# Split-weight stores issued by GpSimd instead of SyncE, and a scan that writes its own first column instead of a GpSimd copy

## The chip, the cores and the metric

The kernel runs on one core of a Trainium2 chip. A core has five engines, each with its own queue of instructions that it works through in order: TensorE (PE in the profile; its weight loads are PEld), VectorE (DVE), ScalarE (ACT), GpSimd (POOL) and SyncE (SP, which here only issues DMAs). Engines wait for one another through semaphores. DMAs move data between HBM and the on-chip memory SBUF; matmuls write to PSUM. A DMA is issued by an engine's queue (here SyncE, ScalarE or GpSimd) and runs beside the engines. The metric is device time in microseconds (us) of one execution; lower is better.

## The reference

A two-layer decoder trunk on x of 2048 positions by 1024 channels, float32. Layer 0 is a gated short convolution, layer 1 a stick-breaking attention with 8 heads of 64:

```python
def _short_conv_mixer(h, w_in, w_conv, w_out):
    u = h @ w_in                                   # 1024 -> 4096
    b_gate, c_gate, xin, g = jnp.split(u, 4, axis=-1)
    y = b_gate * _causal_depthwise_conv(c_gate * xin, w_conv)   # width 3
    return (y * jax.nn.silu(g)) @ w_out

# attention, per block of 128 queries
z = jnp.einsum("bhqd,bhkd->bhqk", qb, kf[:, :, :kl]) * scale
mask = jnp.arange(kl)[None, :] < q_pos[:, None]
log_one_minus = jnp.where(mask, jax.nn.log_sigmoid(-z), 0.0)
rev = lax.cumsum(log_one_minus, axis=3, reverse=True)
weights = jnp.exp(jnp.where(mask, z + rev, -jnp.inf))
outs.append(jnp.einsum("bhqk,bhkd->bhqd", weights, vf[:, :, :kl]))
```

The whole is: x plus mixer of RMSNorm(x); k and v from a RMSNorm of that; q and a SiLU gate from another RMSNorm; x plus the gated attention output times w_out_b; a last RMSNorm. Since exp(z + rev) is sigmoid(z) times the product of sigmoid(−z) over the later keys, a weight is one sigmoid times a running product. The kernel stores positions in reverse, so the running product goes from the low column to the high one.

## The kernel before

Channels lie on the 128 partitions, positions in four chunks of 512 columns (`CH`). Matmuls run in three passes: each weight and each activation is split into a high part (rounded to fp32r) and a low part (the rest), and `mm3` (L205) multiplies high by high, high by low and low by high: 24 matmuls of 128x128 by 128x512 for a depth of 1024.

*Weights.* `load_raw` (L176) loads a block of 128 columns of a weight matrix from HBM, 512 KB, into one of two raw buffers (`NRAW`); its DMA is line L180. `split` (L172) makes the high part on ScalarE (L173) and the low part by a subtraction on VectorE, or on GpSimd for w_out_b (L174). `split_w` (L188) does this into a tile `whl`, one of four (`NWB`), and then writes the split tile, 1 MB (512 KB for w_out_b), to HBM with a DMA on SyncE's queue (L194). Every later use of the block loads the split form back (L202). A block is split once: 8 each for the four gates C, X, B and G of the mixer, 8 each for w_kv and w_in_b (`fold_gains`, which multiplies the norm's gain in first, L366), 8 for w_out_a and 8 for w_out_b, 64 in all. A `whl` buffer is free again when its matmuls are done and its store has landed; a raw buffer is free when its split is done.

*Mixer.* `mixer_in` goes over 8 blocks of channels; for each it computes the gates C, X, B, G of one chunk, or of chunks 0 and 1 together in the first stage, in which all those weights are split. One such block for two chunks is called a round in the prediction. The convolution's tile `p` takes two extra columns from the chunk before: GpSimd copies them in from `halo` (L334) and out to it (L335). The squares for the first norms of chunks 0 and 1 are summed on GpSimd (L170).

*Attention.* `attention(c, h, ot)` handles chunk c of queries and head h; it goes over key chunks `kc` from c down to 0 and over four blocks `qi` of 128 queries. ScalarE makes R = sigmoid(−z) (L489) and w = sigmoid(z) (L491) from PSUM. R is one of five buffers (`NR`) of 513 columns: columns 1 to 512 hold sigmoid(−z), column 0 the product carried in. On the diagonal (kc = c) GpSimd masks R and w (L495) and sets the first column to 1 (L497); off the diagonal it copies the carry, the last column of the R of the key chunk before, into column 0 (L499). VectorE turns columns 1 to 512 into running products with a scan (L500) and multiplies w by R shifted by one column (L504). Then TensorE transposes w (L512), ScalarE and VectorE split the result into `wth` and `wtl` (L173, L174), and TensorE multiplies both by v into `av` (L521, L522). With five buffers, the R of one scan takes the buffer of the R whose last column served as carry to the scan just ahead.

*Out.* `gated` multiplies by the gate on GpSimd (L568), `out_b` projects with w_out_b, adds the residual on VectorE (L591) and sums squares on GpSimd (L170), `out_norm` scales the result on GpSimd (L610).

*Order.* The work is written as Python generators that `merge` interleaves by planned costs; a scheduler then fixes each engine's order from its own timing model of the program as built. Each queue keeps that order on the chip, so an instruction that waits holds up everything behind it on the same engine. Stages follow one another: the mixer of chunks 0 and 1 with all weight splits (to about 400 us), then projections of one chunk beside the mixer of the next and attention of earlier chunks (to about 1400 us), then attention of the last chunk beside the out projections.

Of the kernel before, what the change touches and what calls it, by code (L numbers as in the profile page):

```python
# [8 lines left out]
F32 = mybir.dt.float32  # L9
# [3 lines left out]
ALU = mybir.AluOpType  # L13

P = 128
# [4 lines left out]
CH = 512  # L20
# [25 lines left out]
def kernel(  # L46
# [15 lines left out]
    nc = tc.nc  # L62
# [8 lines left out]
    ones = const.tile([P, P], F32, name="ones")  # L71
# [100 lines left out]
    def split(hi, lo, src, eng=nc.vector):  # L172
        nc.scalar.copy(hi, src)  # L173
        eng.tensor_sub(lo, src, hi.bitcast(F32))  # L174
# [8 lines left out]
    def w_tile(nm, kt=KD):  # L183
        return sb.tile([P, 2, kt, P], F32R, name=f"whl_{nm}", tag="whl", bufs=NWB)


    split_d = {}

    def split_w(raw, key, nm, kt=KD, eng=nc.vector):

        wt = w_tile(nm, kt)
        split(wt[:, 0], wt[:, 1], raw, eng)
        split_d[key] = dram.tile([P, 2, kt, P], F32, name=f"sw_{nm}")
        nc.sync.dma_start(out=split_d[key], in_=wt.bitcast(F32))  # L194
        return wt

    def load_w(src, key, nm, kt=KD, eng=nc.vector):

        if key not in split_d:
            return split_w(load_raw(src, nm, kt), key, nm, kt, eng)  # L200
        wt = w_tile(nm, kt)
        nc.sync.dma_start(out=wt.bitcast(F32), in_=split_d[key])  # L202
        return wt
# [157 lines left out]
    def fold_gains():  # L361

        for nm, src, gain in (("kv", w_kv, gains["kv"]), ("b", w_in_b[0], gains["b"])):
            for i in range(KD):
                raw = load_raw(src[:, i * P:(i + 1) * P], f"fold_{nm}{i}")
                nc.vector.tensor_mul(raw, raw, gain.unsqueeze(2).to_broadcast([P, KD, P]))  # L366
                split_w(raw, (nm, i), f"{nm}{i}")
                yield 1.0
# [96 lines left out]
    def attention(c, h, ot):  # L465

        hb, hi_ = divmod(h, 2)
        nm0 = f"{c}_{h}"
        q2 = sb.tile([P, 2, CH], F32R, name=f"q2_{nm0}", tag="q2", bufs=2)
        for i in range(2):  # L470
            nc.scalar.dma_start(out=q2[i * 64:(i + 1) * 64, :, :].bitcast(F32), in_=q_d[c][hb][hi_ * 64:(hi_ + 1) * 64, :, :])
        av = psum.tile([P, CH], F32, name=f"av_{nm0}", tag="av", bufs=NAV)
        carry = [None] * 4
        for kc in range(c, -1, -1):
            nm = f"{nm0}_{kc}"
            diag = kc == c
            kt = sb.tile([P, CH], F32R, name=f"kt_{nm}", tag="kt", bufs=2)
            nc.scalar.dma_start(out=kt.bitcast(F32), in_=k_d[kc][h])
            vt = sb.tile([P, 4, 2, 64], F32R, name=f"vv_{nm}", tag="vv", bufs=2)
            nc.scalar.dma_start(out=vt.bitcast(F32), in_=v_d[kc][:, :, h, :, :])  # L480
            ws = []
            for qi in range(4):
                lo = qi * P if diag else 0
                lom = min(lo, 256)
                ps = psum.tile([P, CH], F32, name=f"z_{nm}_{qi}", tag="z", bufs=NZ)
                nc.tensor.matmul(ps[:, lom:CH], q2[:, 0, qi * P:(qi + 1) * P], kt[:, lom:CH], start=True, stop=False)  # L486
                nc.tensor.matmul(ps[:, lom:CH], q2[:, 1, qi * P:(qi + 1) * P], kt[:, lom:CH], start=False, stop=True)
                R = sb.tile([P, CH + 1], F32, name=f"R_{nm}_{qi}", tag="R", bufs=NR)
                nc.scalar.activation(R[:, lo + 1:CH + 1], ps[:, lo:CH], AF.Sigmoid, scale=-0.125)  # L489
                w = sb.tile([P, CH], F32, name=f"w_{nm}_{qi}", tag="w", bufs=NW)  # L490
                nc.scalar.activation(w[:, lo:CH], ps[:, lo:CH], AF.Sigmoid, scale=0.125)  # L491
                if diag:

                    for blk, fill in ((R[:, lo + 1:lo + 1 + P], 1.0), (w[:, lo:lo + P], 0.0)):
                        nc.gpsimd.affine_select(out=blk, in_=blk, pattern=[[1, P]], base=0, channel_multiplier=-1,  # L495
                                                compare_op=ALU.is_gt, fill=fill)
                    nc.gpsimd.memset(R[:, lo:lo + 1], 1.0)  # L497
                else:
                    nc.gpsimd.tensor_copy(R[:, 0:1], carry[qi])  # L499
                nc.vector.tensor_tensor_scan(out=R[:, lo + 1:CH + 1], data0=R[:, lo + 1:CH + 1],  # L500
                                             data1=ones[:, 0:1].to_broadcast([P, CH - lo]),
                                             initial=R[:, lo:lo + 1] if diag else carry[qi], op0=ALU.mult, op1=ALU.mult)
                carry[qi] = R[:, CH:CH + 1]
                nc.vector.tensor_mul(w[:, lo:CH], w[:, lo:CH], R[:, lo:CH])  # L504
                ws.append(w)
                yield (1400.0 if diag else 1800.0) / 4
            for kb in range(3, -1, -1):
                nq = kb + 1 if diag else 4
                n = max(256, nq * P)
                wt = psum.tile([P, CH], F32, name=f"wt_{nm}_{kb}", tag="wt", bufs=NWT)  # L510
                for qi in range(nq):
                    nc.tensor.transpose(wt[:, qi * P:(qi + 1) * P], ws[qi][:, kb * P:(kb + 1) * P], ident)  # L512
                first, final = diag and kb == 3, kc == 0 and kb == 0
                wh = sb.tile([P, CH], F32R, name=f"wth_{nm}_{kb}", tag="wth", bufs=NWTS)
                wl = sb.tile([P, CH], F32R, name=f"wtl_{nm}_{kb}", tag="wtl", bufs=NWTS)
                if nq == 1:
                    nc.gpsimd.memset(wh[:, P:2 * P].bitcast(F32), 0.0)
                    nc.gpsimd.memset(wl[:, P:2 * P].bitcast(F32), 0.0)
                split(wh[:, 0:nq * P], wl[:, 0:nq * P], wt[:, 0:nq * P])
                vs = vt[:, kb, :, :].rearrange("p a d -> p (a d)")  # L520
                nc.tensor.matmul(av[:, 0:n], vs, wh[:, 0:n], start=first, stop=False)  # L521
                ins = nc.tensor.matmul(av[:, 0:n], vs, wl[:, 0:n], start=False, stop=final)  # L522
                anchors.append(ins)
                if kb:
                    yield (1900.0 if diag else 3500.0) / 4
            if kc == 0:
                osl = slice(hi_ * 64, hi_ * 64 + 64)
                oth = slice(64 - hi_ * 64, 128 - hi_ * 64)
                nc.scalar.copy(ot[osl, :], av[oth, :])
                nc.vector.tensor_add(ot[osl, :], ot[osl, :], av[osl, :])  # L530
            yield (1900.0 if diag else 3500.0) / 4

    def attention_chunk(c, gated=True):
        for hb in range(NH // 2):
            ot = sb.tile([P, CH], F32, name=f"ot_{c}_{hb}", tag="ot", bufs=2)
            yield from attention(c, 2 * hb, ot)
            yield from attention(c, 2 * hb + 1, ot)
            nc.sync.dma_start(out=og_d[c][hb], in_=ot)
# [168 lines left out]
    def heads(lo, hi, c):  # L707
        for hb in range(lo, hi):
            ot = sb.tile([P, CH], F32, name=f"ot_{c}_{hb}", tag="ot", bufs=2)
            yield from attention(c, 2 * hb, ot)  # L710
            yield from attention(c, 2 * hb + 1, ot)
            if hb == 3:
                last_ot.append(ot)
            else:
                nc.sync.dma_start(out=og_d[c][hb], in_=ot)
# [15 lines left out]
    lo, hi = range(0, NB), range(NB, KD)  # L731
# [34 lines left out]
```

## Time and profile before

| quantity | value |
|---|---|
| median of 3 runs | 1909.28 us (1908.41 to 1910.37) |
| profiled execution | 1907.57 us, its span 1905.8 us |
| TensorE busy | 1784.0 us, 94% of the span |
| VectorE busy | 1264.6 us, 66% |
| ScalarE busy | 769.7 us, 40% |
| GpSimd busy | 436.2 us, 23% |
| carry copies L499 on GpSimd | 192, 112.3 us |
| scans L500 on VectorE | 320, 372.7 us |
| chain that ended last | TensorE 69%, VectorE 14%, DMA 9%, ScalarE 2%, GpSimd 1% |

The profile is one execution, taken by the hardware profiler; its times are counted from the start of the span. A row of the windows view gives, for one stretch of time, the busy time and the number of instructions of each engine, the clock granted to TensorE, the share of DMA capacity used and GB/s. A row of the waits view says which instruction waited for which: total us, times, longest. A row of the chain of work gives start, duration and the work that was on the path. In rows of groups, `out<-in` names the tiles, then shape, count, busy time, mean ns of one, and idle time before them with what ended it. Where a row has three numbers with slashes, they are the shortest, median and longest duration in ns. In rows of DMA issues the last number is the median time from issue to landing in us.

### The profile page before, as it was taken

Reading aid. Unit: us, or ns where it says so; the run is one execution under the profiler, and the core shown is the slowest. Engines: PE = TensorE matmul, PEld = TensorE weight load, DVE = VectorE, ACT = ScalarE, POOL = GpSimd, SP = SyncE. Lnnn points to the kernel's source line nnn. Section 1 sums busy time; section 2 is a strip of 40 time slices with the busy share of each in tenths; the row PEclk is TensorE's granted clock in tenths of the full one; section 3 lists DMA queues with packets and bytes.
Section 4 is the critical chain, followed back from the end, with each engine's and each line's share of the span. In section 5 each row is a group of like instructions: output and inputs, shape, how many; then the busy total and the mean of one; then the engine's idle time right before and its main releaser. Section 6 shows DMA issues by size and latency. Waiting matters only on the chain.

```text
span 1905.8 us, 24702 instructions
## 1 busy us (share of the span) xinstructions
PE 1784.0 (94%) x8312; PEld 1449.4 (76%) x8312; DVE 1264.6 (66%) x1895; ACT 769.7 (40%) x1481; POOL 436.2 (23%) x822
## 2 busy tenths in 40 slices
PE   7899999999999999999999999999979999878785
PEld 5787777778888888888788888888857788656563
DVE  7644554574334264428888346788897999999996
ACT  6312222241123133314545233444555666565553
POOL 5000000000011021103123112222422224654641
PEclk9999999999999999999999999999999999999897
DMA  9648787798887779776767776655746665877751
GB/s 314 210 150 248 248 254 237 243 312 304 295 284 270 258 237 286 246 262 224 242 211 268 238 253 219 202 175 197 258 144 196 197 199 193 284 225 250 252 177 50
DMA packets 226702, 443.64 MB, mean 233 GB/s; under 512 B 16912, under 2 KB 131600, under 8 KB 199952
## 3 DMA queue, kind: packets, MB, share of 16 engines
q1 hardware_dynamic: 166496, 383.30, 60.0%
q10 hardware_dynamic: 59920, 58.74, 10.9%
q8 instruction: 66, 1.08, 0.2%
q14 instruction: 60, 0.49, 0.1%
q0 software_dynamic: 160, 0.02, 0.1%
HBM read 314.34 MB, written 127.66 MB: 232 GB/s over the span
## 4 chain that ended last, share of the span: by engine, by line
PE 69%; DVE 14%; DMA 9%; issue 4%; ACT 2%; POOL 1%; SPq 0%; ACTq 0%; POOLq 0%; DVEq 0%
PE pX L216 8%; PE po L216 7%; PE pG L216 7%; PE pC L216 7%; PE pB L216 6%; PE pg L216 5%; PE pk L216 5%; PE pq L216 5%; PE pv L216 4%; PE wt L512 4%; DVE R L500 4%; PE av L522 3%; DVE w L504 2%; PE av L521 2%; PE z L486 2%
## 5 line engine op out<-in xcount | busy, mean ns | idle before, releaser
L500 DVE TENSOR_TENSOR_SCAN R<-R,R,ones 128x512 f32<-128x512 f32 x192 | 256.6, 1339 | 11.4 <-ACT R L489 11.1
L489 ACT ACTIVATE R<-z 128x512 f32<-128x512 f32 (+1 forms) x320 | 174.2, 544 | 173.1 <-DVE R L500 78.4
L174 DVE TENSOR_TENSOR wtl<-wt,wth 128x512 fp32r<-128x512 f32 (+1 forms) x320 | 185.6, 600 | 67.2 <-ACT wth L173 66.3
L504 DVE TENSOR_TENSOR w<-w,R 128x512 f32<-128x512 f32 (+1 forms) x320 | 212.2, 671 | 21.3 <-POOL R L499 3.0
L173 ACT CAST wth<-wt 128x512 fp32r<-128x512 f32 (+1 forms) x320 | 160.3, 526 | 160.1 <-PE wt L512 137.4
L216 PE MATMUL pC<-h,whl_C 128*128 128x512 f32 x768 | 197.1, 405 | 14.4 <-ACT whl_C L173 8.3
L216 PE MATMUL pG<-h,whl_G 128*128 128x512 f32 x768 | 186.6, 393 | 9.9 <-ACT whl_G L173 9.9
L499 POOL COPY R<-R 128x1 f32<-128x1 f32 x192 | 112.3, 585 | 360.8 <-DVE R L500 293.3
L216 PE MATMUL pX<-h,whl_X 128*128 128x512 f32 x768 | 187.6, 393 | 6.0 <-ACT cs L320 3.9
L216 PE MATMUL po<-y,whl_o 128*128 128x512 f32 x768 | 187.8, 394 | 2.0 <-DVE x L389 1.3
L512 PE MATMUL wt<-ident,w 128*128 128x128 f32 x1088 | 177.8, 278 | 9.2 <-DVE w L504 5.1
L216 PEld LDWEIGHTS pC<-h,whl_C 128*128 128x128 f32 x768 | 148.2, 195 | 49.4 <-ACT whl_C L173 8.3
L216 PE MATMUL pB<-h,whl_B 128*128 128x512 f32 x768 | 185.6, 392 | 0.0
L216 PEld LDWEIGHTS pG<-h,whl_G 128*128 128x128 f32 x768 | 143.2, 188 | 41.0 <-ACT whl_G L173 11.6
L491 ACT ACTIVATE w<-z 128x512 f32<-128x512 f32 (+1 forms) x320 | 172.7, 543 | 0.5 <-PE wt L512 0.5
L216 PEld LDWEIGHTS pX<-h,whl_X 128*128 128x128 f32 x768 | 142.2, 188 | 37.6 <-ACT cs L320 5.1
L216 PEld LDWEIGHTS po<-y,whl_o 128*128 128x128 f32 x768 | 144.2, 189 | 33.5 <-DVE x L389 1.9
L512 PEld LDWEIGHTS wt<-ident,w 128*128 128x128 f32 x1088 | 138.6, 143 | 38.3 <-DVE w L504 7.2
L216 PEld LDWEIGHTS pB<-h,whl_B 128*128 128x128 f32 x768 | 143.0, 188 | 30.1 <-DVE cv L356 0.4
L522 PE MATMUL av<-wtl,vv 128*128 128x512 f32 (+1 forms) x320 | 129.1, 405 | 36.7 <-DVE wtl L174 36.6
L500 DVE TENSOR_TENSOR_SCAN R<-R,ones 128x512 f32<-128x512 f32 (+3 forms) x128 | 116.1, 913 | 33.8 <-POOL R L495 32.2
L486 PE MATMUL z<-kt,q 128*128 128x512 f32 (+1 forms) x320 | 129.1, 405 | 4.1 <-ACT w L491 3.4
(170 smaller groups left out, 2655.3 us busy)
## 6 DMA issues: line engine op xcount, KB each, us to landing
whl_o<-sw_o SPq DMA_DIRECT2D x24, 1024.0 KB, 5.7
kt<-k_d ACTq DMA_DIRECT2D x80, 256.0 KB, 3.6
vv<-v_d ACTq DMA_DIRECT2D x80, 256.0 KB, 4.0
whl_C<-sw_C SPq DMA_DIRECT2D x16, 1024.0 KB, 5.4
whl_X<-sw_X SPq DMA_DIRECT2D x16, 1024.0 KB, 5.5
whl_B<-sw_B SPq DMA_DIRECT2D x16, 1024.0 KB, 5.5
whl_G<-sw_G SPq DMA_DIRECT2D x16, 1024.0 KB, 5.2
whl_k<-sw_kv SPq DMA_DIRECT2D x16, 1024.0 KB, 5.2
```

The lines of the kernel that those rows point to most:

```text
L173: nc.scalar.copy(hi, src)
L174: eng.tensor_sub(lo, src, hi.bitcast(F32))
L216: ins = nc.tensor.matmul(ps, w[:, k, :], a[:, m, k, :], start=n == 0, stop=n == 3 * kt - 1)
L486: nc.tensor.matmul(ps[:, lom:CH], q2[:, 0, qi * P:(qi + 1) * P], kt[:, lom:CH], start=True, stop=False)
L489: nc.scalar.activation(R[:, lo + 1:CH + 1], ps[:, lo:CH], AF.Sigmoid, scale=-0.125)
L491: nc.scalar.activation(w[:, lo:CH], ps[:, lo:CH], AF.Sigmoid, scale=0.125)
L499: nc.gpsimd.tensor_copy(R[:, 0:1], carry[qi])
L500: nc.vector.tensor_tensor_scan(out=R[:, lo + 1:CH + 1], data0=R[:, lo + 1:CH + 1], data1=ones[:, 0:1].to_broadcast([P, CH - lo]), initial= ...
L504: nc.vector.tensor_mul(w[:, lo:CH], w[:, lo:CH], R[:, lo:CH])
L512: nc.tensor.transpose(wt[:, qi * P:(qi + 1) * P], ws[qi][:, kb * P:(kb + 1) * P], ident)
L521: nc.tensor.matmul(av[:, 0:n], vs, wh[:, 0:n], start=first, stop=False)
L522: ins = nc.tensor.matmul(av[:, 0:n], vs, wl[:, 0:n], start=False, stop=final)
```

## The change

Line 194 issues its DMA on GpSimd's queue. In `attention`, GpSimd sets column 0 of every R to 1, on the diagonal or not, and makes no copy of the carry. The scan covers one column more, from column `lo` in place of `lo + 1`: its initial value (1 on the diagonal, the carry off it) is multiplied by that 1 and written to the first column. The carry is read by the scan alone.

```diff
@@ split_w
         split_d[key] = dram.tile([P, 2, kt, P], F32, name=f"sw_{nm}")
-        nc.sync.dma_start(out=split_d[key], in_=wt.bitcast(F32))
+        nc.gpsimd.dma_start(out=split_d[key], in_=wt.bitcast(F32))
         return wt
@@ attention
-                    nc.gpsimd.memset(R[:, lo:lo + 1], 1.0)
-                else:
-                    nc.gpsimd.tensor_copy(R[:, 0:1], carry[qi])
-                nc.vector.tensor_tensor_scan(out=R[:, lo + 1:CH + 1], data0=R[:, lo + 1:CH + 1],
-                                             data1=ones[:, 0:1].to_broadcast([P, CH - lo]),
-                                             initial=R[:, lo:lo + 1] if diag else carry[qi], op0=ALU.mult, op1=ALU.mult)
+                nc.gpsimd.memset(R[:, lo:lo + 1], 1.0)
+                nc.vector.tensor_tensor_scan(out=R[:, lo:CH + 1], data0=R[:, lo:CH + 1],
+                                             data1=ones[:, 0:1].to_broadcast([P, CH + 1 - lo]),
+                                             initial=1.0 if diag else carry[qi], op0=ALU.mult, op1=ALU.mult)
                 carry[qi] = R[:, CH:CH + 1]
```

## The prediction

> **What bounds the kernel now.** I read the windows of busy time by stage first, then the waits of TensorE in each stage that is not full, then the chain of work through one such wait, and last the rows of the operations that the diff touches.
>
> ```profile
> span 1905.8 us, 24702 instructions
> ```
>
> ```profile
> core 0: us, PE busy (x) PEld busy (x) DVE busy (x) ACT busy (x) POOL busy (x), PEclk, DMA share, GB/s
> 0.00:60.00 60.00, 48.81 (x197) 36.98 (x198) 45.69 (x82) 37.72 (x58) 27.71 (x30) 1.00 1.02 318
> 60.00:130.00 70.00, 63.97 (x279) 52.34 (x278) 35.32 (x73) 14.55 (x22) 2.12 (x5) 0.95 0.59 186
> 130.00:400.00 270.00, 254.70 (x1100) 207.53 (x1099) 139.38 (x163) 65.19 (x80) 12.91 (x27) 0.99 0.75 234
> 400.00:1400.00 1000.00, 995.85 (x4762) 827.35 (x4761) 587.94 (x918) 359.76 (x745) 183.28 (x449) 1.00 0.75 249
> 1400.00:1600.00 200.00, 182.37 (x916) 146.09 (x915) 180.47 (x262) 120.32 (x243) 56.51 (x117) 0.98 0.56 181
> 1600.00:1850.00 250.00, 207.02 (x950) 158.29 (x949) 237.27 (x336) 149.90 (x296) 140.10 (x181) 0.92 0.73 235
> 1850.00:1905.80 55.80, 31.30 (x120) 20.81 (x118) 38.52 (x66) 22.23 (x41) 13.59 (x13) 0.77 0.24 78
> ```
>
> From 400 to 1400 us TensorE is busy 995.85 of 1000 us: nothing that either edit does there to VectorE or GpSimd can move the end. Two stretches are left. From 130 to 400 us TensorE lacks 270 − 254.7 = 15.3 us while VectorE and GpSimd are half empty or emptier. From 1600 to 1850 us VectorE is busy 237.27 of 250 us and TensorE lacks 43 us; there VectorE is the bound. What TensorE waits for in the two:
>
> ```profile
> PE pG L216 <- ACT whl_G L173: 9.9, 4, 2.8
> PE pX L216 <- ACT cs L320: 3.9, 3, 2.5
> ```
>
> ```profile
> PE av L522 <- DVE wtl L174: 32.5, 27, 4.1
> ```
>
> Early it waits four times, 2.5 us each, for the split of the gate weights G. Late it waits for VectorE. The chain that leads to one of the G waits:
>
> ```profile
> 153.35 0.32 SPq L194
> ...
> 153.77 7.78 DMA wr_X<-in_w_in_a_dram
> ...
> 163.99 0.32 SPq L194
> ...
> 164.40 6.45 DMA wr_fold_kv<-in_w_kv_dram
> ...
> 174.51 5.01 DMA sw_kv<-whl_kv
> ...
> 179.62 1.05 ACT whl_G L173
> ...
> 180.72 1.22 PE pG L216 x2
> ```
>
> All of it is transfers and splits: a raw load of 7.8 us, another of 6.5, then a store of 5.0 whose landing frees the weight buffer that G's split writes. Each raw load goes out right behind a store on SyncE's queue (153.35 then 153.77, 163.99 then 164.40). So the store line is in the chain in two ways: its issue and bytes stand ahead of the loads, and its landing ends the chain.
>
> **The change, part by part.** *The stores.* Line 194 issues 64 of them (8 each for C, X, B, G, kv, b, o and ob). All leave SyncE's queue and enter GpSimd's.
>
> ```profile
> SPq L194 <- DVE whl_kv L174: 42.7, 8, 13.5
> SPq L194 <- DVE whl_G L174: 32.8, 5, 6.6
> ```
>
> ```profile
> wr_fold_kv<-in_w_kv_dram SPq DMA_DIRECT2D x8, 512.0 KB, 6.4
> wr_ob<-in_w_out_b_dram SPq DMA_DIRECT2D x8, 256.0 KB, 4.7
> g_a<-in_norm_a_dram ACTq DMA_DIRECT2D x1, 4.0 KB, 4.6
> g_kv<-in_norm_kv_dram POOLq DMA_DIRECT2D x1, 4.0 KB, 7.0
> ```
>
> ```profile
> L79 POOL DMA_DIRECT2D g_kv<-in_norm_kv_dram x1 | 1.0, 1045 | 0.4 <-issue 0.4
> L79 POOL DMA_DIRECT2D g_b<-in_norm_b_dram x1 | 0.9, 886 | 0.0
> ```
>
> SyncE's long waits at line 194 (42.7 us over eight kv splits) do not all become gain: what stands behind each is a raw load that needs one of two raw buffers, and that buffer comes free with the same split. What a load gains is the store's issue, 153.77 − 153.35 = 0.4 us, and the place of 1 MB in the queue ahead of it. I bound the second by the rows: nothing at one end; at the other 6.4 − 4.7 = 1.7 us, as if it landed like the raw ob load, which has half the bytes. I take 0.9, the middle, since nothing stands nearer to either end. Two loads a round: 2 × (0.4 + 0.9) = 2.6 us earlier.
>
> The store itself gets later. A GpSimd issue holds the engine 0.9 to 1.0 us against 0.32 on SyncE, so at least 0.6 us; the nearest landing pair, 4 KB each, is 7.0 against 4.6, so up to 2.4 us (a scattered load in the crowded first microseconds, therefore far). I take 1.5, the middle. A round is then 2.6 − 1.5 = 1.1 us shorter, between −2.4 + 0.8 (1.6 longer) and 4.2 − 0.6 (3.6 shorter). A round, one block of columns for two chunks, is 192 matmuls (2 × 4 × 24), and 1100 stand in 130 to 400 us: five full rounds, four with a G wait of 2.5 us, which is longer than 1.1, so the whole 1.1 counts each time; I count the fifth as half a wait: about −5 us for 4.5 rounds. What is late next is TensorE itself, 15.3 us away at most.
>
> The same stores in GpSimd's own order: in 130 to 400 us it is busy 12.91 of 270 us, and what waits behind a store there are the two-column halo copies, each needed a few microseconds later; nothing, and 1 us per copy if that cover is gone. In 0 to 60 us it is busy 27.71 us, mostly with sums of squares for the first norms; three stores stand between them, so the first norm factor comes up to 3 us later, against transfers (DMA share 1.02) in which loads now overtake stores. I take +1 us, between −2 and +3. The eight ob stores fall at 1574 to 1629 us, among late GpSimd work: 8 × 1 us of an engine with 44% slack, +0.5, up to 8.
>
> *The first column.* 192 copies go, 192 one-column memsets come, and each scan covers 513 columns in place of 512.
>
> ```profile
> L499 POOL COPY R<-R x192: 173/734/1182, 801.3 to 1861.8; 128x1 f32<-128x1 f32 x192
> ```
>
> ```profile
> L497 POOL MEMSET R<- x128: 92/98/101, 22.1 to 1819.5; 128x1 f32 x128
> ```
>
> ```profile
> L500 DVE TENSOR_TENSOR_SCAN R<-R,R,ones 128x512 f32<-128x512 f32 x192 | 256.6, 1339 | 11.4 <-ACT R L489 11.1
> L504 DVE TENSOR_TENSOR w<-w,R 128x512 f32<-128x512 f32 x224 | 170.6, 766 | 19.3 <-POOL R L499 3.0 <-POOL R L497 0.2 <-POOL w L495 0.2
> ```
>
> ```profile
> L500 DVE TENSOR_TENSOR_SCAN R<-R,R,ones x192: 1254/1277/2386, 809.8 to 1865.4; 128x512 f32<-128x512 f32 x192
> ```
>
> ```profile
> L489 ACT ACTIVATE R<-z 128x512 f32<-128x512 f32 (+1 forms) x320 | 174.2, 544 | 173.1 <-DVE R L500 78.4
> ```
>
> The last row is the sigmoid. A copy takes 173 ns at least and 734 in the median; the memset never leaves 92 to 101 ns, though scans and products run beside it. GpSimd is relieved of 112.3 − 192 × 0.098 = 93 us. Of that little is on the path:
>
> ```profile
> 1600.00:1850.00 250.00, 27.23 (x54) 0.92 0.73 235
> ```
>
> only 54 copies, 27.23 us, are in the stretch where VectorE bounds, and VectorE waited for a copy 3.0 us in the whole run. Gain: 3.0 us at most as a wait, and at the other end 54 × 0.173 = 9 us if each copy's own time is taken from VectorE's operands. I take 1. One column more is 192 × 1339/512 ns = 0.5 us, 54 of them in the stretch: 0.1.
>
> The cost is a new wait. So far a non-diagonal scan waited for ScalarE's sigmoid alone, and the copy had the scan's 1.3 us to finish before the product needed it. Now the scan needs the memset, and the memset stands in GpSimd's order. With five buffers for R it may not start before the scan just ahead ends; the sigmoid of 0.54 us runs meanwhile, so 0.1 us is hidden if GpSimd is free. It often is not:
>
> ```profile
> 1838.34 8.36 POOL L610 TENSOR_TENSOR x2r<-x2r,pbs 128x512 f32<-128x512 f32 x5 [3.77 <-ACT pbs L605]
> ```
>
> ```profile
> 1846.99 0.69 DVE L504 TENSOR_TENSOR w<-w,R 128x512 f32<-128x512 f32 x1 [3.03 <-POOL R L499]
> ```
>
> Five products of 1.67 us in a row, and VectorE stood 3.03 us for one copy behind them. In the changed program's order a memset stands behind those same five products, with a scan, one step earlier than the product, behind it. Behind that scan are VectorE's further splits, and TensorE's transposes wait for those. GpSimd without its copies is busy (140.10 − 27.23)/250 = 45% of the stretch in operations of 1.3 to 1.8 us. A scan that meets one waits about half of it less the sigmoid, 0.8 − 0.5 = 0.3 us: 54 × 0.45 × 0.3 = 7 us. Much of this was paid before, since a scan that starts beside such an operation is stretched (1277 ns in the median, 2386 at most); I count a third, +2.5, between 0 and 9 us.
>
> The sum: −5 + 1 + 0.5 − 1 + 0.1 + 2.5 = −1.9 us by the middles. I lean two microseconds lower, because the loads' middle leaves out that they no longer stand behind a store whose split is late, where SyncE lost 13.5 us in one wait; with half a microsecond for each of 4.5 rounds it is −4.2. The profiled execution takes 1907.57 us (span 1905.8 and 1.8 around it), 1.7 below the median of 1909.28; against the median the forecast is 1905.
>
> **The rivals.** (1) *The store's landing decides.* If a GpSimd store lands 2.4 us later and loads gain only the issue, a round is 1.6 us longer, and TensorE pays in all five: +8, with +1.5 elsewhere and late +2.5 − 1 about +11, hence 1920. It decides from a store later by more than the loads gain, 2.6 us at my values. For it speaks that the chain ends in this landing; against it, that the 4 KB pair is far from a plain 1 MB store.
>
> (2) *The memset behind GpSimd's big operations decides*: the full 9 us late, stores −2: 1917. It turns the sign where the new waits are over 5 us. For it speaks the 3.03 us row; against it, that VectorE is stretched by those operations anyway.
>
> (3) *The G waits vanish.* Loads gain 2.1 each and the store 0.6: 3.6 a round exceeds every wait, so the 9.9 us go and some of the 15.3: −12, 1897. The Trainium skill, "DMA: Bandwidth & Descriptors", section "Anatomy of one DMA — SWDGE (gpsimd) path", fits such a DMA at 2.0 us plus bytes over 436 GB/s, an estimate of 4.4 us for 1 MB, against the 5.0 that SyncE's store takes here; by that figure the store would not be later at all. No run here shows a GpSimd store of that size.
>
> (4) *VectorE holds up the stores' issue.* VectorE is busy 139.38 of 270 us in operations of 0.86 us on average. If every issue waits out what runs, a store is later by up to 1.2 us more, a split's length: a round gains nothing and the time is about 1910. The Trainium skill, "SBUF — State Buffer", section "SBUF: two separate sides", has this mechanism: GpSimd cannot write a DMA's descriptors while VectorE holds the ports that they share. By it issues would read well over 1 us; GpSimd's few DMAs of this trace, two of them in the rows above, stand before VectorE's work, so the trace shows neither.
>
> (5) *Both edits are hidden*: the round's time is set by what does not change, and the time is 1909.
>
> **How the numbers follow.** A measurement here tells 0.2%, 3.8 us, from no change. Forecast 0.40, own range 1900 to 1910: 0.26 faster, 0.13 same, 0.01 slower. Rival 1 0.18 (0.17 slower, 0.01 same), rival 2 0.16 (0.15 slower, 0.01 same), rival 3 0.18 (all faster), rival 4 0.04 (0.03 same, 0.01 slower), rival 5 0.04 (same). Faster 0.44, same 0.22, slower 0.34. The range from 1893 to 1921 leaves out the far halves of the outer cases.
>
> **What would show it.** Right: whl_G waits of TensorE in 130 to 400 us fall from 9.9 to about 5 us, raw loads land in 5.5 us rather than 6.4, sw stores in about 6.5 rather than 5.0; memsets stay near 0.1 us; VectorE waits at the scan for GpSimd's R a few microseconds in 1600 to 1850 us. Wrong: whl_G waits that name the store grow (rival 1); scan waits above 9 us (rival 2); TensorE above 99% in 130 to 400 us (rival 3). The whole order of instructions is computed anew from the changed program, so a few microseconds may also come from matmuls standing otherwise, which no row prices.

## The result, and the profile after

The changed kernel takes 1952.84 us in the median of four runs (1950.74 to 1957.38), the kernel before 1909.67 (1908.41 to 1910.37) beside it: 43.2 us slower, ratio 1.023 with a 95% interval of 1.0209 to 1.0251. The prediction said 1905, faster; the time lies above its range too. The profiled execution takes 1957.38 us, the slowest of the four (span 1955.7).

The windows of busy time of the changed kernel, in the columns shown before:

```profile
130.00:400.00 270.00, 244.48 (x1025) 196.86 (x1024) 124.22 (x146) 54.85 (x66) 27.32 (x57) 0.96 0.61 217
400.00:1400.00 1000.00, 989.81 (x4687) 820.84 (x4686) 571.68 (x893) 350.69 (x720) 149.90 (x442) 0.99 0.74 248
1600.00:1850.00 250.00, 212.96 (x967) 163.70 (x966) 227.47 (x304) 143.43 (x284) 108.12 (x176) 0.92 0.71 231
```

From 130 to 400 us TensorE does 1025 matmuls where it did 1100. At 231.5 ns each (254.70 / 1100) the missing 75 are 17 us. Where the stage ends is seen in the tile view: the matmuls of the first output projection, with their first and last start, in the kernel before:

```profile
L216 PE MATMUL po<-y,whl_o x192: 387/389/497, 400.2 to 456.3; 128*128 128x512 f32 x192
```

and in the changed kernel:

```profile
L216 PE MATMUL po<-y,whl_o x192: 388/389/794, 426.6 to 486.5; 128*128 128x512 f32 x192
```

So 30 us (486.5 − 456.3) are lost before 487 us, in the stage that splits and stores weights. The rest comes later, most of it after 1400 us: the matmul that starts at 1400.7 us in the kernel before, counted in order, starts at 1433.8 in the changed one, 33.1 later, and the two profiled spans end 49.9 us apart (43.2 in the medians). What TensorE waits for from 130 to 400 us, in the changed kernel:

```profile
PE pX L216 <- DVE cv L356: 14.6, 5, 3.7
PE pG L216 <- ACT whl_G L173: 5.9, 3, 3.4
```

and the wait for line L356 in the kernel before:

```profile
PE pX L216 <- DVE cv L356: 1.5, 1, 1.5
```

G's waits fell from 9.9 to 5.9 us, as predicted, and yet the stage is longer: the wait for line L356 on VectorE grew from 1.5 to 14.6 us and took their place. The chain of work through one round of the changed kernel tells why; its columns are start, duration and what ran:

```profile
308.66 6.77 DMA sw_b<-whl_b
...
317.87 9.58 DMA wr_B<-in_w_in_a_dram
...
327.56 1.06 ACT whl_B L173
...
328.64 0.50 DVE whl_B L174
...
335.01 8.33 DMA sw_b<-whl_b
...
343.41 1.05 ACT whl_G L173
...
344.50 0.73 PE pG L216 x2
```

There are two stores in it, of 6.8 and 8.3 us, and a raw load of 9.6. VectorE stands at the split of B until that load has landed; the product of L356 is behind the split in its order, and TensorE's X matmuls need what that product frees. ScalarE holds it up in the same way: the sigmoid of L351, which the product needs, stands behind B's cast (L173). The DMA issues of the changed kernel, with KB each and the median from issue to landing:

```profile
sw_kv<-whl_kv POOLq DMA_DIRECT2D x8, 1024.0 KB, 7.6
sw_G<-whl_G POOLq DMA_DIRECT2D x8, 1024.0 KB, 7.1
sw_b<-whl_b POOLq DMA_DIRECT2D x8, 1024.0 KB, 7.2
wr_X<-in_w_in_a_dram SPq DMA_DIRECT2D x8, 512.0 KB, 5.5
wr_B<-in_w_in_a_dram SPq DMA_DIRECT2D x8, 512.0 KB, 9.6
```

And of the kernel before:

```profile
sw_kv<-whl_kv SPq DMA_DIRECT2D x8, 1024.0 KB, 5.0
sw_G<-whl_G SPq DMA_DIRECT2D x8, 1024.0 KB, 5.0
sw_b<-whl_b SPq DMA_DIRECT2D x8, 1024.0 KB, 5.0
wr_X<-in_w_in_a_dram SPq DMA_DIRECT2D x8, 512.0 KB, 6.4
wr_B<-in_w_in_a_dram SPq DMA_DIRECT2D x8, 512.0 KB, 6.7
```

These three groups of stores land 2.1 to 2.6 us later. The loads of X land 0.9 earlier, as predicted, and those of B 2.9 later. Of the others, C's land 1.2 earlier and those for kv and b 0.3 and 0.6; G's land as before (7.4 against 7.3).

### The profile page after: what moved, and what is told of

It is laid out like the page before. It is cut to its first block, busy times and chain, and to the rows that moved or that the text cites. A ratio compares the mean times of both kernels' runs of the same rounds, so it can differ in the third digit from the quotient of the medians.

```text
span 1955.7 us, 24772 instructions
## 1 busy us (share of the span) xinstructions
PE 1812.0 (93%) x8312; PEld 1464.8 (75%) x8312; DVE 1264.3 (65%) x1895; ACT 768.2 (39%) x1481; POOL 380.7 (19%) x886
## 4 chain that ended last, share of the span: by engine, by line
PE 60%; DVE 13%; DMA 9%; issue 5%; ACT 3%; POOL 1%; ACTq 0%; POOLq 0%; DVEq 0%; SPq 0%
PE po L216 8%; PE pC L216 6%; PE pG L216 6%; PE pX L216 5%; PE pB L216 5%; DVE R L498 5%; PE pg L216 4%; PE wt L510 4%; PE pk L216 4%; PE pq L216 4%; PE pv L216 4%; PE av L520 2%; DVE w L502 2%; PE av L519 2%; PE z L486 2%
## 5 line engine op out<-in xcount | busy, mean ns | idle before, releaser
L498 DVE TENSOR_TENSOR_SCAN R<-R,R,ones 128x513 f32<-128x513 f32 x192 | 258.8, 1350 | 23.4 <-ACT R L489 18.3
L173 ACT CAST wth<-wt 128x512 fp32r<-128x512 f32 (+1 forms) x320 | 161.1, 528 | 162.8 <-PE wt L510 136.1
L216 PE MATMUL pX<-h,whl_X 128*128 128x512 f32 x768 | 197.5, 407 | 24.7 <-DVE cv L356 17.7
L216 PEld LDWEIGHTS pX<-h,whl_X 128*128 128x128 f32 x768 | 148.3, 196 | 61.0 <-issue 20.0
L519 PE MATMUL av<-wth,vv 128*128 128x512 f32 (+1 forms) x320 | 125.1, 391 | 8.3 <-ACT wth L173 6.2
L498 DVE TENSOR_TENSOR_SCAN R<-R,ones 128x513 f32<-128x513 f32 (+3 forms) x128 | 109.7, 862 | 32.0 <-POOL R L495 30.2
```

The lines of the kernel that those rows point to most:

```text
L216: ins = nc.tensor.matmul(ps, w[:, k, :], a[:, m, k, :], start=n == 0, stop=n == 3 * kt - 1)
L498: nc.vector.tensor_tensor_scan(out=R[:, lo:CH + 1], data0=R[:, lo:CH + 1], data1=ones[:, 0:1].to_broadcast([P, CH + 1 - lo]), initial=1.0 ...
```

## The experiments

Two theories were open for the early loss: (A) the stores' queue itself is slower, (B) the order of all instructions, computed anew for the changed program, is worse. For the late loss there was a third, that the memset's wait costs it.

**Each edit alone.** Line 194 alone, then the first column alone:

```diff
-        nc.sync.dma_start(out=split_d[key], in_=wt.bitcast(F32))
+        nc.gpsimd.dma_start(out=split_d[key], in_=wt.bitcast(F32))
```

> Only line 194 is changed: the 64 stores of split weights go out on GpSimd's queue; the attention's copies and scans are those of the kernel before, and the order of instructions is computed anew for it. If the stores are behind the 30 us that the changed kernel has lost by 460 us, this kernel loses those 30: about 1940. If the late loss of some 13 us (1400 us to the end) is theirs too, through the eight ob stores in GpSimd's queue, about 1952. If the stores are innocent, 1910.

> Only the first column is changed: 192 memsets in place of 192 copies, scans of 513 columns; the stores stay on SyncE. If the memset's wait behind GpSimd's long operations is what costs 13 us after 1400 us, about 1922 and the loss lies after 1400 us. If the copies' going is a gain as I priced it, or nothing, 1905 to 1912.

stores_only takes 1937.89 us, 30.6 more than the kernel before (ratio 1.0174, 1.0154 to 1.0194); column_only 1915.79, 8.5 more (1.0054, 1.0037 to 1.0071), between its two expectations. Both edits lose, and 39 of the 43 us are their sum. The stores are the larger part. Each of these runs has an order of its own, so each figure holds an edit and an order.

**The same order.** To part queue and order, the program is built twice. The first build is the kernel before; its order on each engine is then laid on the second build, which has the edit, by edges that only fix the order and make nothing wait. Only the 64 stores are free to stand where they fit; in the traces those that stay on SyncE stand where they did. Two lines are added ahead, so L196 is the store and L175 the cast. The edit, cut to its main lines:

```diff
+        for name in order:
+            ins = traced[name]
+            if ins.name in STORES:
+                continue
+            e = str(ins.engine)
+            if e in last:
+                tc.add_manual_dep(ins, last[e], PACE, reason="held order")
+            last[e] = name
...
+    nc, traced = build(['sync', False])
+    order = [i.name for f in nc.m.functions for blk in f.blocks for i in blk.instructions if i.name in traced]
+    nc, traced = build(['gpsimd', False], order)
```

> The 64 stores go out on GpSimd's queue, and every other instruction of every engine stands in exactly the order that it has in the kernel before. Theory A (the queue itself: a store lands some 2 us later, a weight buffer comes free later, loads share the wires with stores): nearly the whole loss of the first 460 us stays, 1930 to 1945. Rival B (the order computed anew, which puts splits ahead of the work that TensorE waits for): little stays, 1905 to 1915.

> The mirror of the run before it: the 64 stores are issued by SyncE as in the kernel before, and every other instruction stands in the order computed for stores on GpSimd. Theory A (the queue itself): 1905 to 1915. Rival B (the order): 1930 to 1945. If both this and its mirror lose, the two add up.

stores_held_order takes 1933.3 us, 26.0 more (1.0133, 1.0089 to 1.0177). syncE_new_order takes 1944.84, 37.5 more (1.021, 1.0188 to 1.0232). Neither theory has it alone: the slow queue costs 26 us in an order made for SyncE, and the order made for GpSimd's queue costs 37 with the stores on SyncE. They do not add up: the new order with the queue that it was made for, as in stores_only, costs 31. So the new order was no gain with either queue; beside GpSimd's the difference of 5 us lies within the scatter of stores_held_order. What goes with the new order is the wait for L356 (L358 here): it is there in stores_only,

```profile
PE pX L216 <- DVE cv L356: 16.9, 5, 4.2
```

and in syncE_new_order, where no store is on GpSimd:

```profile
PE pX L218 <- DVE cv L358: 15.8, 3, 6.1
```

With the order held, the queue's own harm can be read. TensorE's waits from 130 to 400 us in stores_held_order:

```profile
PE pG L218 <- ACT whl_G L175: 16.3, 4, 5.0
PE pX L218 <- DVE cv L358: 6.1, 1, 6.1
PE pX L218 <- ACT cs L322: 1.4, 2, 0.7
```

G's four waits grew from 9.9 to 16.3 us, 1.6 each. The chain into the first of them in stores_held_order:

```profile
175.29 1.24 DVE whl_kv L176
176.52 0.28 issue
176.81 7.00 DMA sw_kv<-whl_kv
...
183.88 1.05 ACT whl_G L175
...
184.97 1.22 PE pG L218 x2
```

It is the chain that the prediction showed, with a landing 7.29 us after the split in place of 5.01 (179.52 − 174.51). The windows view of the stage, in the columns shown before:

```profile
130.00:400.00 270.00, 246.24 (x1027) 200.50 (x1026) 124.72 (x146) 55.83 (x66) 27.21 (x57) 0.94 0.62 217
```

TensorE lacks 73 matmuls, 17 us. The waits account for 23.8 − 15.3 = 8.5 us of them. The rest is the clock. A windows view of the slices around this wait and the next, in stores_held_order (TensorE's busy time and matmuls, then the granted clock, DMA share, GB/s):

```profile
180.00:190.00 10.00, 5.03 (x12) 0.66 0.48 161
...
230.00:240.00 10.00, 6.09 (x20) 0.71 0.48 165
```

and the slices with the same two waits in the kernel before:

```profile
180.00:190.00 10.00, 9.28 (x34) 0.83 0.58 173
...
220.00:230.00 10.00, 7.42 (x34) 1.00 0.83 255
```

The 0.66 and 0.71 are means of a slice. In the trace the clock is either full or half, and after the first of these waits the matmuls start 0.43 us apart until 189.8 us, then 0.23. Each of the five longest waits of stores_held_order, 2.9 to 6.1 us, comes with 6.8 us at half clock, 34 us in the stage. In the same stage of the kernel before, two of the six waits of 1.5 to 2.8 us come with 3.4 us each, the other four with none. Over the stage a matmul takes 246.24 / 1027 = 239.8 ns against 231.5: 8.4 us for 1027 of them. The Trainium skill, "TensorE: Matmul & The Clock Gate", section "What's actually happening", has the array at half rate once an activity window of some 3.4 us was idle. The half rate is in the traces; the 3.4 us are no sharp limit here, since waits of 2.1, 2.8 and 2.9 us came with half clock too.

**Any second queue, or GpSimd's?** The stores on ScalarE's queue, order held (the theory C of this expectation is GpSimd's own way of sending):

```diff
+    nc, traced = build(['scalar', False], order)
```

> The 64 stores go out on ScalarE's queue, and every other instruction stands in the order of the kernel before. Theory C (GpSimd's own way of sending: 0.53 us to issue, 7 to 8 us to land against 5): on ScalarE's queue a store lands after some 5 us as on SyncE's, and the loss goes: 1905 to 1914. Rival D (any second queue: loads and stores that no longer stand in one line share the wires, and the stores that free the weight buffers land later for it): the stores land after 6.5 us or more and 15 to 25 us are lost, 1922 to 1932.

1917.6 us, 9.8 more (1.0045, 1.003 to 1.006), between the two expectations. Most of the loss is gone; from 130 to 400 us G's waits are those of the kernel before:

```profile
PE pG L218 <- ACT whl_G L175: 10.1, 4, 3.0
```

Its DMA issues show the stores that count landing nearly as on SyncE, though the loads no longer stand behind them:

```profile
sw_G<-whl_G ACTq DMA_DIRECT2D x8, 1024.0 KB, 5.6
sw_kv<-whl_kv ACTq DMA_DIRECT2D x8, 1024.0 KB, 5.4
sw_b<-whl_b ACTq DMA_DIRECT2D x8, 1024.0 KB, 5.5
```

So a second queue costs about 10 us, ScalarE's own issuing included (4 of them are lost in the first 61 us), and some 16 of the 26 go with GpSimd's queue itself. The DMA packets in the traces show where its 2 us lie: before the first packet. Of the eight 1 MB stores in stores_held_order that had GpSimd's queue to themselves, the first packet moved 3.0 to 3.4 us after the issue, and the transfer then took 3.1 to 3.4 us. From ScalarE the first packet moved some 2.1 us after the issue; from SyncE, with G's stores, 0.8.

**Which stores?** Only the 16 folded stores, kv and b, go back to SyncE:

```diff
-        STORES.add(getattr(nc, MODE[0]).dma_start(out=split_d[key], in_=wt.bitcast(F32)).ins.name)
+        STORES.add(getattr(nc, "sync" if key[0] in ("kv", "b") else MODE[0]).dma_start(out=split_d[key], in_=wt.bitcast(F32)).ins.name)
```

> As stores_held_order, but the 16 stores of folded weights (kv, b), the ones whose landing ends the chain to G's splits, stay on SyncE; the other 48 go out on GpSimd; order of the kernel before. If the landing of the folded stores is the cost, most of the 26 us of stores_held_order goes: 1906 to 1915. If the stores of C, X, B and G carry the cost, 1922 to 1932.

1913.39 us, 4.5 more (1.0033, 1.0017 to 1.0049). The stores of C, X, B, G and o still land after 6.9 to 8.3 us there, and it hardly matters. By the difference, the 16 whose landing frees the buffer of G's splits carry 21 of the 26 us.

**A fifth weight buffer.** If it is the buffer that is waited for, more buffers should end the waits:

```diff
-NR, NW, NT, NL, NWB, NRAW, NWTS = 5, 8, 4, 5, 4, 2, 2
+NR, NW, NT, NL, NWB, NRAW, NWTS = 5, 8, 3, 4, 5, 2, 1
```

> The kernel before with five weight buffers in place of four; the room comes from the pools t (3 for 4), ld (4 for 5) and wth/wtl (1 for 2), so the attention, from 460 us on, will be slower by tens of us, and only the time to the end of the first output projection (456.6 us before) is compared with its partner. If the release of weight buffers by landed stores is what TensorE waits for early, G's waits (9.9 us) go and that projection ends at 440 to 452 us.

> Its partner: the same pools, the stores on GpSimd's queue. If the loss comes because a weight buffer is freed only when its store has landed, a fifth buffer hides the later landing, and the first output projection ends within 8 us of its partner's. If the loss comes from shared wires or from the order, it stays 20 to 30 us behind.

Both are slower in all (1993.58 and 2029.6 us), as was expected of pools that gave up room. The stage itself is what was asked for. With the stores on SyncE TensorE is full from 130 to 400 us:

```profile
130.00:400.00 270.00, 270.00 (x1193) 223.43 (x1192) 155.60 (x193) 73.57 (x93) 12.49 (x25) 1.00 0.84 267
```

The output projection's last matmul starts at 432.0 us, 24 earlier than in the kernel before and earlier than expected. With the stores on GpSimd it starts at 458.2, 26 behind its partner: the expectation of 8 was missed. The two have different orders, so this pair cannot tell the queue from the order. With the stores on GpSimd too no wait for G is left, only one for L356:

```profile
PE pX L216 <- DVE cv L356: 12.1, 4, 3.7
```

**Two spare buffers.** The 16 folded splits get two buffers in the space of the tile `og`, idle until the first output projection, so that nothing gives up room. The order is computed anew for spare_syncE, and spare_gpsimd_held holds that order:

```diff
-    def split_w(raw, key, nm, kt=KD, eng=nc.vector):
-        wt = w_tile(nm, kt)
+    def split_w(raw, key, nm, kt=KD, eng=nc.vector, wt=None):
+        if wt is None:
+            wt = w_tile(nm, kt)
...
+        spare = sb.tile([P, 2, 2, KD, P], F32R, name="fold", tag="og", bufs=1)
...
-                split_w(raw, (nm, i), f"{nm}{i}")
+                split_w(raw, (nm, i), f"{nm}{i}", wt=spare[:, i % 2])
```

> The kernel before (stores on SyncE), but the 16 folded splits (kv and b) go into two weight buffers of their own, which take the space of the tile og, idle until the first output projection; nothing else gives up room. The four weight buffers are left to C, X, B and G. If TensorE's early waits come from weight buffers that are freed late, TensorE is full from 130 to 400 us as with five buffers, and the time falls by about 20 us: 1883 to 1893. If the buffers of C, X, B and G are not short for the folded ones, 1903 to 1910.

> The same, with all 64 stores on GpSimd's queue and every other instruction in the order of spare_syncE. If the queue's harm is only that a buffer comes free later, it now has room: within 6 us of spare_syncE. If GpSimd's queue harms in another way too (raw loads slowed by sharing, late issue), it is 15 us or more behind it.

spare_syncE takes 1895.73 us, 13.2 less than the kernel before (0.993, 0.991 to 0.995): it beats both kernels. The 13 us are those of the buffers and of the new order together; no run parts them. From 130 to 400 us no wait for G is left, and the longest of TensorE's waits is

```profile
PE pX L216 <- DVE cv L356: 2.6, 2, 2.4
```

The gain is under the expected 20: the projection's last matmul starts at 440.5 us, 16 earlier, and some of that is lost again later. spare_gpsimd_held, with every store on GpSimd's queue, takes 1902.17 (0.9971, 0.9955 to 0.9988), 6.4 more than its partner, just over the 6 expected, and still faster than the kernel before. Its projection, by the tile view:

```profile
L218 PE MATMUL po<-y,whl_o x192: 388/389/767, 382.4 to 443.7; 128*128 128x512 f32 x192
```

The last start is 3.2 us behind spare_syncE's, where stores_held_order was 22.8 behind the kernel before (479.1 − 456.3):

```profile
L218 PE MATMUL po<-y,whl_o x192: 387/389/500, 423.1 to 479.1; 128*128 128x512 f32 x192
```

The stores land just as late (7.0 us for kv and b); with a buffer to spare TensorE hardly waits for it (0.3 us for a split of G from 130 to 400 us).

**The late part.** The first column alone, each memset at the place of the copy that it replaces (L500 is the memset here, L501 the scan):

```diff
+    nc, traced = build(['sync', False])
...
+    nc, traced = build(['sync', True], order)
```

> The first column alone, as in column_only, with every instruction in the order of the kernel before (each memset at the place of the copy it replaces). If the memset's wait is the cost, the 8 us of column_only stay: 1914 to 1918. If the order computed anew was the cost, 1905 to 1910.

1912.45 us, 4.6 more (1.0023, 1.0009 to 1.0037): half of column_only's 8.5, and between the two expectations. What VectorE waits for from 1600 to 1850 us:

```profile
DVE R L501 <- POOL R L500: 6.5, 2, 5.0
```

In the kernel before the waits for GpSimd there were 3.0 us, once, for a copy. The chain shows the long one at the very place that the prediction named:

```profile
1842.15 4.77 POOL x2r L619 x3
1846.92 0.18 issue
1847.11 2.48 POOL x2r L619 x2
1849.59 0.14 POOL wth L526
1849.73 0.04 POOL R L500
1849.77 0.02 issue
1849.80 1.29 DVE R L501
```

Five products of the output on GpSimd, a short memset of another tile (L526), then the memset, then the scan.

In the changed kernel itself, with its own order, this wait is not there. From 1600 to 1850 us VectorE waits for no memset, and from 1400 us to the end it does so twice (L497 is the memset, L498 the scan):

```profile
DVE R L498 <- POOL R L497: 2.8, 2, 1.7
```

Last, the eight ob stores alone on GpSimd (the first line), and both edits together (the second), each in the order of the kernel before:

```diff
+        STORES.add(getattr(nc, MODE[0] if key[0] == "ob" else "sync").dma_start(out=split_d[key], in_=wt.bitcast(F32)).ins.name)
...
+    nc, traced = build(['gpsimd', True], order)
```

> The kernel before with only the eight ob stores (512 KB each, 1574 to 1629 us) on GpSimd's queue, order of the kernel before. If they carry what stores_held_order loses after 1400 us (22.7 us behind at 1400, 26.6 at the end), 1911 to 1914. If they cost nothing, 1907 to 1910, and that late difference is scatter.

> Both edits, with every other instruction in the order of the kernel before. If the two edits add up and the rest of the changed kernel's loss is the order computed anew, the sum of stores_held_order (26) and column_held_order (4.6): about 1938, some 14 us under the changed kernel. If the two hurt each other late (the memsets stand behind GpSimd's stores of ob), about the changed kernel's time, 1948 to 1955.

ob_store_held_order takes 1912.95 us, 4.5 more (1.0027, 1.0015 to 1.0039). With the 21 us of the folded stores that makes up the 26 of stores_held_order, within their scatter. Which wait carries these 4.5 was not isolated. both_held_order takes 1934.09, 25.7 more (1.0138, 1.0107 to 1.017); the sum of the parts was 30.6, within the scatter of stores_held_order (1921.39 to 1938.21). The changed kernel is 1.023 against 1.0138: some 17 us of its 43 are the order computed anew, some 26 the two edits themselves. In the profiled runs some 11 us of the order's share lie before 1400 us, where the wait for L356 is; what the later part waits for was not isolated.

## Why the prediction was wrong

*The stores, predicted −5, measured +26 with the order held.* The chain was the right one, and its last link, the landing that frees G's buffer, is what decides: rival 1. The step that failed is the sum of the round, 1.1 us shorter by the prediction; with the order held, each of G's waits is 1.6 us longer. Three of its terms were mis-sized.

- The loads' gain of 0.4 + 0.9 us each. The 0.9 was not there: in stores_held_order the medians of C, X, B, G, kv and b average 6.7 us, against 6.6 before, C's 1.1 earlier and B's 1.9 later. A load that no longer stands behind a store can go out beside it. Of these loads from 60 to 430 us, 18 of 40 met at most 0.4 MB of GpSimd's traffic on their way and landed in 4.5 to 5.1 us; the 19 slowest, 6.8 to 12.1 us, met 1.25 MB or more. So the upper end of 1.7 came true for nearly half of them, and the others lost about as much.
- The store's landing of +1.5 us. It is +1.8 to +1.9 for kv and b in stores_held_order, where they hold G, and +2.2 to +2.6 in the changed kernel. The upper end, 2.4, was near; the 4 KB pair, called far, was not far off. GpSimd's issue holds it 0.53 us, not the 0.9 to 1.0 of the gain loads.
- The price of a longer wait, taken one for one. Each of G's waits grew by 1.6 us, the very figure of rival 1, which made +8 of five of them. The clock that falls with the longer waits cost about as much again, and the wait for L358 (L356 before) grew from 1.5 to 6.1 us. So rival 1, too, was a third of what the stage loses (22.8 us to the end of the projection).

The further lean of −2 us, for loads that no longer stand behind a late split, is priced by no run alone; the loads as a whole gained nothing. The +1 us for the first 60 us was about right: in the profiled runs stores_held_order is 0.8 us behind after 200 matmuls, at 61 us. The eight ob stores, +0.5 us taken and up to 8 allowed, measured +4.5.

*The order.* The prediction's last sentence gave it a few microseconds and no price. It is some 17 us of the changed kernel. In the early chain of the changed kernel it is the split of B standing ahead of L356 on VectorE, which made the mark "whl_G waits fall to about 5 us" come true (5.9) while the stage got longer.

*The first column, predicted +1.6 in all, measured +4.6 with the order held.* Memsets of 98 ns and a scan of 513 columns in 1340 ns (1339 before) are as priced. The new wait is 6.5 us where 3.0 went, within the range of 0 to 9 but above the 2.5 taken: rival 2 has the right mechanism, at half its price. In the changed kernel's own order that wait is absent, so the mark set for it, a few microseconds from 1600 to 1850 us, did not come true there.

*Rival 3* fell: by the Trainium skill, "DMA: Bandwidth & Descriptors", section "Anatomy of one DMA — SWDGE (gpsimd) path", a 1 MB transfer would have taken an estimated 4.4 us, and the medians for kv, G and b are 6.8 to 7.6 from GpSimd. The same page's table "Issuing engine by pattern" puts plain stores on SyncE, with which the runs agree. *Rival 4* fell too: no issue takes over 0.6 us, where it needs well over 1. Nor does VectorE hold up what follows the issue: in stores_only and the changed kernel the first packet of a lone GpSimd store moved 2.9 to 3.3 us after an issue with VectorE idle, in stores_held_order 3.1 to 3.4 with VectorE busy for 90% or more of those 3 us. *Rival 5* fell with the result.

## What to carry to other kernels

Before a DMA is moved to another queue, find who waits for it to land: a store that nobody waits for can land 2 us later for nothing, one that frees a buffer costs that in every round. If the chain ends in a buffer's release, look for another buffer first; here the space of a tile idle in that stage gave two; with the order computed for them the kernel was 0.7% faster, and GpSimd's queue cost 6 us in place of 26. Where a scheduler orders the program, hold the order fixed in one run, or an edit's price and the new order's price cannot be told apart.

## What was not expected of the hardware

A plain 1 MB store of kv, G or b issued by GpSimd landed some 7 us after its issue in the median, from SyncE 5.0, from ScalarE 5.4 to 5.6, in the same order of instructions. GpSimd's first packet moved 3.0 to 3.4 us after the issue, SyncE's 0.8. Waits of TensorE that grew from 2.5 to 4 or 5 us cost about twice what they grew by (8.5 us of waits, 8.4 us of slower matmuls in the stage), since each came with 6.8 us at half clock; of the waits of 1.5 to 2.8 us, two of six came with 3.4 us.
